# Layer 1's gate and up products in seven half-size products for eight, and adaLN columns moved beside down products and merges

## The chip, the cores and the metric

The kernel runs on one core of one Trainium2 chip. The metric is the device time of one execution in microseconds (us), as the median of several runs. A profiled execution gives the trace from which rows are read. The engines are named as the profile names them: PE (TensorE), PEld (its weight loads), DVE (VectorE), ACT (ScalarE), POOL (GpSimd), SP (SyncE, which issues most transfers).

## The reference

Two layers run over 640 tokens of width 1024: 128 context tokens and 512 latent tokens, with shared weights. Scale, shift and gate of each sublayer (adaLN) come from one vector for the context and one for the latents, by a product with `w_mod` (9 x 1024 columns a layer). Everything is float32.

```
h = rms(x, g_pre0) * (1 + c0) + s0
x = x + 0.5 * g0 * rms((silu(h @ Wg0) * (h @ Wu0)) @ Wd0, g_post0)
h = rms(x, g_pre1) * (1 + c1) + s1
x = x + g1 * rms(mixer(h), g_post1)
h = rms(x, g_pre2) * (1 + c2) + s2
x = x + 0.5 * g2 * rms((silu(h @ Wg1) * (h @ Wu1)) @ Wd1, g_post2)
```

Wg and Wu are 1024 x 2816, Wd is 2816 x 1024. The mixer holds a gated linear recurrence, an S5 state space branch and windowed attention; three gated branches are merged and multiplied by `w_out`.

## The kernel before

**Products.** Every large product is made in three matmuls (`mm3`, lines 91 to 95): each operand is split (`split`, lines 97 to 101) into a rounded high part, by a ScalarE cast (L100), and the rest, by a VectorE subtraction (L101), and high x high, high x low and low x high are summed in PSUM. A weight slab of 128 x 1024 (512 KB) is loaded by SP (`slab`, line 72) and split in two halves of 512 columns; six pairs of buffers hold split halves ahead of their use.

**The FFN** (`ffn`, lines 400 to 472). The 2816 hidden columns are 22 blocks of 128. For each block gate and up are made with the hidden columns on the partitions and the tokens as moving columns, in two parts of 384 and 256 tokens (`HALF`), 8 k-tiles each. tanh, two VectorE steps (L434, L435) and a split make the hidden block. The blocks come in two phases of 11; after each, the down product sums 11 blocks into five PSUM banks (five token tiles of 128), for one half of 512 output columns after the other. The first phase's sums are copied by ScalarE to an SBUF tile, `part`; the second phase's are added to it.

```
            for nh in range(2):
                ps = [self.mm() for _ in range(NT)]
                STG = self.STG[0] if (ch == 1 and nh == 1) else 0
                for jj in range(JC - STG):
```

**From one sublayer to the next.** In the last half (`nh == 1`) the last `STG` weight halves (8 in the FFN, 7 in the mixer) are held back, and then used token tile by token tile, so that a tile is finished while PE works on the next. For a finished tile `post_half` (lines 368 to 378) adds the part, squares (L376) and multiplies by the gate row (L377); `post` (from line 380) adds to x (L387; for tiles 2 to 4 half of it by ScalarE and POOL, L389 and L390); `prenorm` (lines 305 to 316) squares x (L310), takes the root on POOL (L300), multiplies by the row `A` = (1 + c) g_pre (L313 on VectorE, L314 on ScalarE, L315 on POOL); `turn` transposes the tile on PE (L327), adds the shift and splits it into the next sublayer's h (L331, L337, L338). The turns of tiles 3 and 4 wait until the next sublayer's first gate and up products of 384 tokens are under way (`flush`, line 348); one more gate product stands behind it.

**adaLN.** `mod_tile` (lines 247 to 258) loads 128 columns of `w_mod` (512 KB) and makes their dot products with the two SiLU rows on VectorE, four multiply-and-sum instructions over 512 elements (L255, each with a read of the accumulator) and two small additions (L258). `rows` (line 264) turns gate and scale columns into rows through a transpose, a DRAM tensor and two POOL transfers. `plan` (lines 500 to 511) lays the columns on the 22 gate and up steps of each FFN (48 in each layer's first FFN, 24 and 8 in the second ones); in layer 0 the S5 preparation lies on the same steps. `silu_rows` makes the SiLU rows anew in each of the four FFNs.

**Order.** Instructions are written in program order, and a planner with a cost model then orders them on each engine; the order on SP is kept as written. Every engine works its queue in order, so an instruction that waits holds up those behind it. Buffers are rings: `pp` (22 tiles of 128 x 640), `hp` (h), `wp`, `bg` (two tiles of 128 x 1024, which hold `w_mod` columns and normalized tiles), `xp`, `rawp`.

## Time and profile before

| | us |
|---|---|
| median of 3 runs | 3217.41 (3217.2 to 3219.97) |
| the profiled execution | 3221.69 |
| its span in the trace | 3219.9 |
| PE busy in the span | 3115.6 |
| DVE busy | 2006.3 |
| ACT busy | 1246.0 |
| POOL busy | 664.8 |

The span runs from the first to the last instruction; the execution's own time is 1.8 us longer. The rows below come from that one execution. A busy time on PE is modelled from pipelined matmuls, so what one matmul costs in a stream is read from the starts of many. Times of stretches are counted from the span's start. The span's order is: layer 0 first FFN to about 525, mixer to 1140, second FFN to 1635; layer 1 first FFN to 2107, mixer to 2721, second FFN to the end.

### The profile page before, as it was taken

How to read it: one execution, taken by the hardware profiler on the slowest of the kernel's cores; microseconds unless marked ns; L12 is line 12 of the kernel's file. 1: busy time of each engine (PE TensorE's matmuls, PEld its weight loads, DVE VectorE, ACT ScalarE, POOL GpSimd, SP SyncE). 2: the span in 40 equal slices, each digit the busy share in tenths (PEclk: the TensorE clock that was granted, in tenths of full speed). 3: DMA queues.
4: the chain of work that ended last, by engine and by line, in shares of the span. 5: the costliest groups of instructions: out<-in, count | busy, mean ns of one | idle time of the engine just before them, and what ended most of it. 6: DMA issues, size and time to landing. Idle time of an engine off the chain costs nothing.

```text
span 3219.9 us, 52039 instructions
## 1 busy us (share of the span) xinstructions
PE 3115.6 (97%) x19981; PEld 2908.8 (90%) x19981; DVE 2006.3 (62%) x4548; ACT 1246.0 (39%) x2757; POOL 664.8 (21%) x933
## 2 busy tenths in 40 slices
PE   7889999999999999999999999999999999999998
PEld 6788997879999989989989999977989998998997
DVE  6994886656735479737679648667565444642443
ACT  4222324475634353322252223246655433422232
POOL 2630002119820037200020000020594101100000
PEclk9999999999999999999999999999989999999999
DMA  6355444231452333524445334434215423422222
GB/s 241 116 184 171 158 158 161 82 77 63 95 151 73 125 125 122 193 98 144 149 146 171 130 112 158 157 119 86 76 56 125 129 72 135 148 86 85 86 99 86
DMA packets 138106, 398.45 MB, mean 124 GB/s; under 512 B 34704, under 2 KB 43424, under 8 KB 135424
## 3 DMA queue, kind: packets, MB, share of 16 engines
q1 hardware_dynamic: 127680, 362.37, 34.8%
q0 software_dynamic: 9456, 31.43, 3.0%
q8 instruction: 157, 2.57, 0.3%
q10 hardware_dynamic: 720, 1.31, 0.1%
q14 instruction: 93, 0.76, 0.1%
HBM read 355.77 MB, written 44.40 MB: 124 GB/s over the span
## 4 chain that ended last, share of the span: by engine, by line
PE 80%; DVE 10%; POOL 4%; issue 3%; ACT 2%; DMA 0%; POOLq 0%; DVEq 0%; SPq 0%; ACTq 0%
PE mm L93 24%; PE mm L94 24%; PE mm L95 24%; DVE wlo L101 1%; DVE junk L255 1%; PE mm L1252 1%; DVE x L387 1%; POOL s5t L1019 1%; PE mm L1241 1%; POOL H L1020 1%; POOL s5t L1018 1%; POOL s5t L1017 1%; PE mm L990 1%; ACT n L310 1%; PE mm L1216 1%
## 5 line engine op out<-in xcount | busy, mean ns | idle before, releaser
L94 PE MATMUL mm<-h,whi 128*128 128x384 f32 (+1 forms) x3968 | 1231.3, 311 | 8.8 <-DVE s L296 5.8
L95 PE MATMUL mm<-h,wlo 128*128 128x384 f32 (+1 forms) x3968 | 1230.4, 311 | 8.2 <-DVE wlo L101 8.2
L93 PE MATMUL mm<-h,whi 128*128 128x384 f32 (+1 forms) x3968 | 1229.7, 312 | 5.4 <-ACT h L337 2.0
L101 DVE TENSOR_TENSOR wlo<-raw,whi 128x512 fp32r<-128x512 f32 x780 | 570.7, 735 | 535.8 <-ACT whi L100 529.8
L94 PEld LDWEIGHTS mm<-h,whi 128*128 128x128 f32 x3968 | 758.5, 191 | 11.6 <-DVE s L296 6.5
L100 ACT CAST whi<-raw 128x512 fp32r<-128x512 f32 x780 | 477.2, 619 | 749.5 <-PE mm L95 382.2
L95 PEld LDWEIGHTS mm<-h,wlo 128*128 128x128 f32 x3968 | 757.9, 191 | 9.5 <-DVE wlo L101 9.5
L93 PEld LDWEIGHTS mm<-h,whi 128*128 128x128 f32 x3968 | 756.3, 191 | 10.8 <-ACT h L337 3.0
L93 PE MATMUL mm<-whi,P 128*128 128x512 f32 x980 | 381.6, 391 | 1.9 <-DVE tmp L434 1.9
L94 PE MATMUL mm<-wlo,P 128*128 128x512 f32 x980 | 381.7, 390 | 0.0
L95 PE MATMUL mm<-whi,P 128*128 128x512 f32 x980 | 381.1, 390 | 0.0
L255 DVE SCALAR_TENSOR_TENSOR junk<-wmod,W 128x512 bf16<-128x512 f32 x512 | 357.7, 699 | 10.0 <-DMA wmod<-w_mod 4.1
L281 POOL DMA_DIRECT2D gd<-grow x6 | 3.2, 528 | 1498.5 <-ACT grow L279 1258.2
L100 ACT CAST P<-tmp 128x384 fp32r<-128x384 f32 x192 | 88.2, 460 | 431.1 <-DVE tmp L435 429.7
L93 PEld LDWEIGHTS mm<-whi,P 128*128 128x128 f32 x980 | 184.0, 188 | 40.6 <-DVE tmp L434 2.4
L95 PEld LDWEIGHTS mm<-whi,P 128*128 128x128 f32 x980 | 184.0, 188 | 38.2
L94 PEld LDWEIGHTS mm<-wlo,P 128*128 128x128 f32 x980 | 184.1, 188 | 37.5
L433 ACT ACTIVATE tmp<-mm 128x384 f32<-128x384 f32 (+1 forms) x176 | 76.5, 435 | 224.6 <-PE mm L95 224.5
L95 PE MATMUL mm<-P,wlo 128*128 128x384 f32 (+1 forms) x512 | 158.8, 310 | 0.0
L94 PE MATMUL mm<-P,whi 128*128 128x384 f32 (+1 forms) x512 | 158.1, 309 | 0.0
L93 PE MATMUL mm<-P,whi 128*128 128x384 f32 (+1 forms) x512 | 158.0, 309 | 0.0
L817 DVE SCALAR_TENSOR_TENSOR tmp<-tmp,mm 128x384 f32<-128x384 f32 x64 | 31.0, 485 | 184.9 <-PE mm L95 92.6
(333 smaller groups left out, 4021.4 us busy)
## 6 DMA issues: line engine op xcount, KB each, us to landing
wmod<-w_mod SPq DMA_DIRECT2D x128, 512.0 KB, 3.5
raw<-w_gate SPq DMA_DIRECT2D x88, 512.0 KB, 3.5
raw<-w_up SPq DMA_DIRECT2D x88, 512.0 KB, 3.5
raw<-w_down SPq DMA_DIRECT2D x88, 512.0 KB, 3.5
raw<-w_in_fm SPq DMA_DIRECT2D x72, 512.0 KB, 3.5
xd<-x SPq DMA_DIRECT2D x25, 512.0 KB, 2.6
x<-xd SPq DMA_DIRECT2D x24, 512.0 KB, 4.4
W<-gd POOLq DMA_DIRECT2D x11, 1024.0 KB, 7.0
```

Source lines behind the costliest of these rows:

```text
L93: nc.tensor.matmul(ps, whi, ahi, start=first, stop=False)
L94: nc.tensor.matmul(ps, whi, alo, start=False, stop=False)
L95: nc.tensor.matmul(ps, wlo, ahi, start=False, stop=last)
L100: nc.scalar.copy(hi, src)
L101: return nc.vector.tensor_tensor(lo, src, hi.bitcast(F32), ALU.subtract)
L255: nc.vector.scalar_tensor_tensor(out=jk, in0=w[:, h * 512:(h + 1) * 512], scalar=1.0, in1=rows[c][h], op0=ALU.mult, op1=ALU.mult, accum_ou ...
L310: nc.scalar.activation(n, x, AF.Square, scale=1.0 / 32.0, accum_out=ss)
L387: nc.vector.scalar_tensor_tensor(out=x[:, hs], in0=f[h], scalar=rs, in1=x[:, hs], op0=ALU.mult, op1=ALU.add)
L433: nc.scalar.activation(t, pg[:, :n], AF.Tanh, scale=0.5)
L990: nc.tensor.matmul(pv[:, g], m1[:, g, ri], U[:, 4 * i + g], start=True, stop=True)
L1017: v.tensor_tensor(t[:, 0, :ns], cur, ar, ALU.mult)
L1018: v.tensor_tensor(t[:, 1, :ns], cur[:, :, ::-1], ai, ALU.mult)
```

## The change

- **Gate and up of layer 1.** In both FFNs of layer 1 the weight blocks are taken in 11 pairs. The first pair is computed as before, in parts of 320 tokens. For the other ten, each matrix of 1024 x 256 is cut into 2 x 2 quarters (512 x 128) and the tokens into 2 x 2 quarters (512 x 320), and seven products of quarters or of sums of quarters replace eight (`seven`). The token sums T1, T3, T2 are made on VectorE (`combine`) and T4 in `combine4`. The weight sums are made by accumulating transfers that POOL issues: two while loading (s, A21), two from one SBUF tile to another (A11 + s, A12 + A11). The seven products are added to four results with ScalarE copies and VectorE additions.
- **Three phases.** The second FFN of layer 0 and both of layer 1 take the blocks in phases of 6, 8 and 8. The sums of the first two phases are copied to SBUF (`put`), written and accumulated in DRAM by POOL, and read back in the last. Before a sublayer with paired products `STG` is 6 (`stage`), and at most one less than the phase's blocks.
- **adaLN columns.** In layer 1, 24 columns of the first FFN stand at the 28 down steps of its first two phases, 24 at the merges of two branches, and the last 8 (and the LRU output) at the second FFN's down steps (`spread`). A column is made by two instructions over 1024 elements for four over 512. The SiLU rows are made once.
- **Norms.** `prenorm` multiplies by the root alone; `turn` applies scale and shift as columns after the transpose. Turns of tiles 0 to 2 are issued two tiles later (`turn_next`), those of 3 and 4 at the next `flush`. `rows` makes the gate rows alone, by four smaller transfers into `pp` tiles.
- **Buffers.** h lies in `wp`, now 7 tiles; the memory for the descriptors of POOL's transfers is set to 8192.

```diff
+PHASES = {(0, 0): (11, 11), (0, 1): (6, 8, 8), (1, 0): (6, 8, 8), (1, 1): (6, 8, 8)}
+PAIRED = ((1, 0), (1, 1))
+PLAIN = tuple((l, i) for l in range(2) for i in range(2) if (l, i) not in PAIRED)
...
-        self.hp = pool("hp", 4)
         self.pp = pool("pp", 22)
-        self.wp = pool("wp", 3)
+        self.wp = pool("wp", 7)
...
-        rows = []
-        w = self.W_()
+        w = self.cp.tile([P, 2, 1024], F32, name="srows")
...
     def mod_tile(self, l, col, rows):
...
-        acc = self.S_(4)
+        m = self.mod[l]["mm"][:, :, col]
         for c in range(2):
-            for h in range(2):
-                jk = self.sm.tile([P, 512], BF16, tag="junk", name=self.nm("junk"), bufs=1)
-                nc.vector.scalar_tensor_tensor(out=jk, in0=w[:, h * 512:(h + 1) * 512], scalar=1.0,
-                                               in1=rows[c][h], op0=ALU.mult, op1=ALU.mult,
-                                               accum_out=acc[:, 2 * c + h:2 * c + h + 1])
-            nc.vector.scalar_tensor_tensor(out=self.mod[l]["m"][c][:, col:col + 1], in0=acc[:, 2 * c:2 * c + 1],
-                                           scalar=acc[:, 2 * c + 1:2 * c + 2], in1=self.mod[l]["b"][:, col:col + 1],
-                                           op0=ALU.add, op1=ALU.add)
+            jk = self.small("junk").bitcast(BF16)
+            nc.vector.scalar_tensor_tensor(out=jk, in0=w, scalar=1.0, in1=rows[:, c], op0=ALU.mult, op1=ALU.mult,
+                                           accum_out=m[:, c:c + 1])
+        nc.vector.tensor_tensor(m, m, self.mod[l]["b"][:, col:col + 1].to_broadcast([P, 2]), ALU.add)
...
+        nc.tensor.transpose(ps[:16, :P], s, self.ident)
...
+        nc.gpsimd.dma_start(d.rearrange("c (k p) -> (c k) p", p=P), g[:16])
+        out["G"] = []
+        for c in range(2):
+            w = [self.P_(shape=[P, 512]) for _ in range(2)]
+            for h in range(2):
+                nc.gpsimd.dma_start(w[h], d[c:c + 1, 512 * h:512 * h + 512].to_broadcast([P, 512]))
+            out["G"].append(w)
         return out
...
+        sq = nc.scalar.activation(n, x, AF.Square, scale=1.0 / 32.0, accum_out=ss)
         rs = self.rstd(ss)
-        self.norm = (
-            v.scalar_tensor_tensor(out=n[:, :512], in0=x[:, :512], scalar=rs, in1=R["A"][ci][0], op0=ALU.mult, op1=ALU.mult),
-            nc.scalar.mul(n[:, 512:], x[:, 512:], rs))
-        self.last_n = nc.gpsimd.tensor_tensor(n[:, 512:], n[:, 512:], R["A"][ci][1], ALU.mult)
-        self.turn(t, n, R, hT)
+        self.norm = (v.tensor_scalar(n, x, rs, None, ALU.mult), sq)
+        def turn():
+            self.turn(t, n, R, hT)
+        (self.turns if t < 3 else self.late).append(turn)
...
+    def turn_next(self, t):
+        if t >= 2 and self.turns:
+            self.turns.pop(0)()
...
+                nc.tensor.transpose(ps[:, i * P:(i + 1) * P], n[:, (4 * q + i) * P:(4 * q + i + 1) * P], self.ident)
+            h = n[:, q * 512:(q + 1) * 512].rearrange("p (k t) -> p k t", k=4)
+            for i in range(4):
+                k = slice(4 * q + i, 4 * q + i + 1)
+                o = ps[:, i * P:(i + 1) * P]
+                if i % 2:
+                    v.tensor_scalar(h[:, i], o, a[:, k], b[:, k], ALU.mult, ALU.add)
+                else:
+                    nc.scalar.activation(h[:, i], o, AF.Identity, scale=a[:, k], bias=b[:, k])
+            hs.append(h)
...
-                for i in range(4):
-                    o, b = ps[:, i * P:(i + 1) * P], B[:, 4 * q + i:4 * q + i + 1]
-                    nc.scalar.activation(hi[:, i], o, AF.Identity, bias=b)
-                    d = v.scalar_tensor_tensor(out=lo[:, i], in0=o, scalar=b, in1=hi[:, i].bitcast(F32),
-                                               op0=ALU.add, op1=ALU.subtract)
-            if t < 3:
-                self.turned = d
+                d = self.split(hi, lo, h)
+        if hT.paired:
+            for c, n_, half, o in self.PIECES[t]:
+                h, cs = [h[:, :, c:c + n_] for h in hs], slice(o, o + n_)
+                d = self.quarters(hT, h, half, cs)
+                if half:
+                    self.todo.append(lambda h=h, cs=cs: self.combine(hT, h, cs))
+            if t == 2:
+                self.combos()
...
+    PIECES = {0: [(0, 128, 0, 0)], 1: [(0, 128, 0, 128)], 2: [(0, 64, 0, 256), (64, 64, 1, 0)],
+              3: [(0, 128, 1, 64)], 4: [(0, 128, 1, 192)]}
...
+    def combine(self, hT, hs, cs):
+        v = self.nc.vector
+        T = {k: (z[:, 0, :, cs], z[:, 1, :, cs]) for k, z in hT.t.items()}
+        h12, h22 = hs
+        n = cs.stop - cs.start
+        t1 = self.tmp.tile([P, 512], F32, tag="tmp", name=self.nm("tc"))[:, :4 * n].rearrange("p (k t) -> p k t", k=4)
+        f = lambda x: x.bitcast(F32)
+        v.tensor_tensor(t1, f(T["B11"][0]), h12, ALU.subtract)
+        v.tensor_tensor(t1, t1, f(T["B11"][1]), ALU.add)
+        self.split(*T["T1"], t1)
+        v.tensor_tensor(h12, h22, h12, ALU.subtract)
+        self.split(*T["T3"], h12)
+        v.tensor_tensor(t1, t1, h22, ALU.add)
+        self.split(*T["T2"], t1, -1.0)
+    def combine4(self, hT):
+        v = self.nc.vector
+        t, f = hT.t, lambda x: x.bitcast(F32)
+        del t["B12"]
+        z = t["T4"] = self.wp.tile([P, 2, 4, TH], F32R, tag="W", name=self.nm("hT4"))
+        for y in range(2):
+            k = slice(2 * y, 2 * y + 2)
+            w = self.P_().rearrange("p (k t) -> p k t", k=2)
+            v.tensor_tensor(w, f(t["T2"][:, 0, k]), f(t["B21"][:, 0, k]), ALU.add)
+            v.tensor_tensor(w, w, f(t["T2"][:, 1, k]), ALU.add)
+            v.tensor_tensor(w, w, f(t["B21"][:, 1, k]), ALU.add)
...
-                STG = self.STG[0] if (ch == 1 and nh == 1) else 0
-                for jj in range(JC - STG):
...
+                STG = min(n - 1, self.stage(self.STG[0], hTn)) if (final and nh == 1) else 0
+                for jj in range(n - STG):
...
+                    if dram and final and nh == 0 and jj == 0:
+                        part = self.new_part()
+                        for t in range(NT):
+                            nc.gpsimd.dma_start(part[t].whole, self.pd[t])
...
+                    self.background(("down", ch, nh, jj))
...
-                    if ch == 0:
-                        nc.scalar.copy(part[t][nh], ps[t])
-                    else:
+                        jj = n - STG + r
+                        self.mm3(ps[t], hid[jj][0][:, ts], hid[jj][1][:, ts], whi, wlo, jj == 0, jj == n - 1)
+                    if final:
...
+    def put(self, t, nh, ps, ch):
+        nc = self.nc
+        k = (5 * nh + t) % 4
+        o = (self.xp if k % 2 else self.bg).tile([P, 512], F32, tag="x" if k % 2 else "bg", name=self.nm("put"))
+        nc.scalar.copy(o, ps)
+        d = self.pd[t][:, nh * 512:nh * 512 + 512]
+        if ch:
+            nc.gpsimd.dma_start(d, o, accum_op=ALU.add)
+        else:
+            nc.gpsimd.dma_start(d, o)
...
+    def paired(self, l, i, hT):
...
+        first(0, 0, 0)
+        first(0, 1, 0)
+        self.flush()
+        product(0, 0)
+        first(1, 0, 0)
+        first(1, 1, 0)
+        product(1, 0)
+        for f in range(2):
+            first(f, 0, 1)
+            first(f, 1, 1)
+            product(f, 1)
+            self.combos()
+        self.combine4(hT)
+        st = [self.rawp.tile([P, 1024], F32, tag="raw", name=self.nm("raw")) for _ in range(2)] + [self.P_(shape=[P, 512])]
+        extra = self.seven(W[0, 1], st, hT.t)
+        next(extra)
+        yield hid[0]
+        yield hid[1]
...
+        sets = [[big[:, o:o + 1024], big[:, o + 1024:o + 2048], big[:, o + 2048:o + 2560]] for o in (0, 2560)]
...
+                    g = self.seven(W[m, jp], sets[m], hT.t)
+                    next(g)
+                out = next(g)
...
+                        if m == 0:
+                            t = self.tmp.tile([P, 512], F32, tag="tmp", name=self.nm("tmp"))[:, :TH]
+                            nc.scalar.activation(t, z, AF.Tanh, scale=-0.5 if f else 0.5)
+                            v.scalar_tensor_tensor(out=z, in0=t, scalar=1.0, in1=z, op0=ALU.add, op1=ALU.mult)
+                        else:
+                            y = gate[f][:, h * TH:(h + 1) * TH]
+                            v.scalar_tensor_tensor(out=z, in0=z, scalar=0.5, in1=y, op0=ALU.mult, op1=ALU.mult)
+                            self.prod = self.split(*(x[:, h * TH:(h + 1) * TH] for x in hid[f]), z)
...
+    def seven(self, src, st, T):
+        nc, v, g = self.nc, self.nc.vector, self.nc.gpsimd
+        x, y, s = st
+        a11, a12, a21, a22 = x[:, :512], x[:, 512:], y[:, :512], y[:, 512:]
+        add = lambda o, a: g.dma_start(o, a, accum_op=ALU.add)
+        nc.sync.dma_start(x, src[:, :1024])
+        nc.sync.dma_start(s, src[:, 1024:1536])
+        self.last_slab = nc.sync.dma_start(y, src[:, 1024:])
+        add(s, src[:, 1536:])
+        add(a21, src[:, :512])
+        yield
+        out = [self.P_(), self.P_()]
+        o = [[z[:, h * TH:(h + 1) * TH] for h in range(2)] for z in out]
+        def product(ps, a, b, more=False):
+            whi, wlo = self.parts(a)
+            for k in range(4):
+                cs = slice(k * P, (k + 1) * P)
+                for e, (w, z) in enumerate(((whi, 0), (whi, 1), (wlo, 0))):
+                    nc.tensor.matmul(ps[:, :TH], w[:, cs], T[b][:, z, k], start=not more and k == e == 0,
+                                     stop=k == 3 and e == 2, skip_group_check=more)
+        yield out
+        pa, pb = self.mm(), self.mm()
+        product(pa, a11, "B11")
+        nc.scalar.copy(o[0][0], pa[:, :TH])
+        add(a11, s)
+        product(pb, a12, "B21")
+        v.tensor_tensor(o[0][0], o[0][0], pb[:, :TH], ALU.add)
+        add(a12, a11)
+        yield [(0, 0)]
+        pe, pf = self.mm(), self.mm()
+        product(pe, s, "T1")
+        nc.scalar.copy(o[1][1], pe[:, :TH])
+        product(pf, a21, "T3")
+        v.tensor_tensor(o[1][1], o[1][1], pf[:, :TH], ALU.add)
+        product(pa, a11, "T2", True)
+        nc.scalar.copy(o[0][1], pa[:, :TH])
+        nc.scalar.copy(o[1][0], pa[:, :TH])
+        v.tensor_tensor(o[1][1], o[1][1], pa[:, :TH], ALU.add)
+        yield [(1, 1)]
+        product(pe, a12, "B22", True)
+        v.tensor_tensor(o[0][1], o[0][1], pe[:, :TH], ALU.add)
+        yield [(0, 1)]
+        product(pf, a22, "T4", True)
+        v.tensor_tensor(o[1][0], o[1][0], pf[:, :TH], ALU.add)
+        yield [(1, 0)]
+    def stage(self, n, hT):
+        return 6 if hT is not None and hT.paired else n
...
+    def spread(self, l, i, fs):
+        slots = [("down", ch, nh, jj) for ch, n in enumerate(PHASES[l, i][:-1]) for nh in range(2) for jj in range(n)]
+        q = {}
+        for k, f in enumerate(fs):
+            q.setdefault(slots[k * len(slots) // len(fs)], []).append(f)
+        return q
...
+                if nh == 1:
+                    self.turn_next(t)
...
+            for f in self.mixq.pop((br, j), ()):
+                f()
...
-            self.plan(self.s5_prep(0) if l == 0 else [], modq(l, range(16, 64)), 0 if l else 3)
+            if (l, 0) in PAIRED:
+                self.bgq = self.spread(l, 0, modq(l, range(16, 40)))
+                self.mixq = {}
+                for x, f in enumerate(modq(l, range(40, 64))):
+                    self.mixq.setdefault((0, x // 2) if x < 16 else (1, x - 16), []).append(f)
+            else:
+                self.plan(self.s5_prep(0), modq(l, range(16, 64)), 3)
...
-                self.plan([(7, self.lru_out)], modq(l, range(64, 72)), 0)
+                self.bgq = self.spread(l, 1, modq(l, range(64, 72)) + [self.lru_out])
...
-    nc = bacc.Bacc("TRN2", target_bir_lowering=False, num_devices=1)
+    nc = bacc.Bacc("TRN2", target_bir_lowering=False, num_devices=1, dynamic_dma_scratch_size=8192)
```

## Rows read from the trace of the kernel before

**Rows 1.** The page's totals: busy us, share of the span, instructions.
```profile
PE 3115.6 (97%) x19981; PEld 2908.8 (90%) x19981; DVE 2006.3 (62%) x4548; ACT 1246.0 (39%) x2757; POOL 664.8 (21%) x933
```

**Rows 2.** Stretches: length, busy us per engine (instructions), granted clock, DMA share, GB/s.
```profile
120.00:240.00 120.00, 104.57 (x871) 99.49 (x872) 119.55 (x255) 32.53 (x75) 48.81 (x41) 0.96 0.51 171
...
1680.00:1800.00 120.00, 120.00 (x821) 120.00 (x820) 106.20 (x294) 38.35 (x75) 0.00 (x0) 1.00 0.50 163
1840.00:1880.00 40.00, 40.00 (x178) 33.11 (x178) 8.30 (x12) 10.33 (x17) 0.00 (x0) 1.00 0.28 93
...
2440.00:2720.00 280.00, 280.00 (x1873) 273.58 (x1872) 121.97 (x225) 107.03 (x219) 33.66 (x66) 1.00 0.40 116
...
1634.00:1674.00 40.00, 34.76 (x174) 30.12 (x174) 34.53 (x64) 24.83 (x56) 18.62 (x18) 0.91 0.52 175
1654.00:1674.00 20.00, 14.76 (x78) 13.50 (x77) 18.53 (x38) 14.70 (x37) 9.98 (x9) 0.83 0.69 219
```

**Rows 3.** PE in order of time, 1700 to 1712: start us, us, line, tiles.
```profile
1701.52 0.28 PE L93 MATMUL mm<-h,whi 128*128 128x256 f32 x1
...
1707.26 0.34 PE L93 MATMUL mm<-h,whi 128*128 128x384 f32 x1
...
1711.95 0.33 PE L93 MATMUL mm<-h,whi 128*128 128x384 f32 x1
```

**Rows 4.** Groups by shape, 3000 to 3080, gate and up: busy us, mean ns.
```profile
L101 DVE TENSOR_TENSOR wlo<-raw,whi 128x512 fp32r<-128x512 f32 x24 | 16.6, 692 | 9.9 <-ACT whi L100 9.9
L255 DVE SCALAR_TENSOR_TENSOR junk<-wmod,W 128x512 bf16<-128x512 f32 x8 | 5.5, 688 | 0.1
L101 DVE TENSOR_TENSOR P<-tmp,P 128x384 fp32r<-128x384 f32 x6 | 3.3, 558 | 3.5 <-ACT P L100 3.5
...
L434 DVE SCALAR_TENSOR_TENSOR tmp<-tmp,mm 128x384 f32<-128x384 f32 x5 | 2.8, 554 | 9.8 <-ACT tmp L433 9.8
...
L101 DVE TENSOR_TENSOR P<-tmp,P 128x256 fp32r<-128x256 f32 x6 | 2.5, 418 | 0.0
L434 DVE SCALAR_TENSOR_TENSOR tmp<-tmp,mm 128x256 f32<-128x256 f32 x6 | 2.5, 412 | 0.0
L258 DVE SCALAR_TENSOR_TENSOR mod<-s,bmod 128x1 f32<-128x1 f32 x4 | 0.9, 216 | 0.1
L255 DVE DVE_READ_ACCUMULATOR junk<-wmod,W 128x1 f32 x8 | 0.7, 82 | 0.0
...
L100 ACT CAST whi<-raw 128x512 fp32r<-128x512 f32 x24 | 14.9, 620 | 14.6 <-PE mm L94 11.2 <-ACT tmp L433 3.4
```

**Rows 5.** Transfers by line: issuing queue, count, KB each, median us to landing.
```profile
raw<-w_gate SPq DMA_DIRECT2D x88, 512.0 KB, 3.5
...
W<-gd POOLq DMA_DIRECT2D x11, 1024.0 KB, 7.0
...
m1d<-W POOLq DMA_DIRECT2D x16, 512.0 KB, 4.8
...
ud<-ut POOLq DMA_DIRECT2D x8, 320.0 KB, 3.2
```

**Rows 6.** Waits of PE, 1610 to 1690: us in total, times, longest.
```profile
PE mm L94 <- DVE h L338: 3.0, 1, 3.0
PE mm L93 <- ACT h L337: 2.0, 1, 2.0
```

**Rows 7.** Groups by shape, 1630 to 1675, a change of sublayer: busy us, mean ns.
```profile
L338 DVE SCALAR_TENSOR_TENSOR h<-mm,mod,h 128x128 fp32r<-128x128 f32 x19 | 5.8, 343 | 0.4 <-ACT h L337 0.3
L101 DVE TENSOR_TENSOR wlo<-raw,whi 128x512 fp32r<-128x512 f32 x6 | 5.4, 932 | 0.2 <-ACT whi L100 0.2
...
L315 POOL TENSOR_TENSOR n<-n,W 128x512 f32<-128x512 f32 x5 | 6.9, 1385 | 2.6 <-ACT n L314 2.6
```

**Rows 8.** Line L255 alone (VectorE), 120 to 240: length, busy us (instructions), clock, DMA, GB/s.
```profile
120.00:240.00 120.00, 44.51 (x111) 0.96 0.51 171
```

More of the change, by code (lines that the diff above doesn't have):

```diff
@@ new lines, in rows @@
+            a = self.sm.tile([P, 2, 8], F32, tag="acol", name=self.nm("acol"), bufs=2)
+            for c in range(2):
+                v.scalar_tensor_tensor(out=a[:, c], in0=self.mod[l]["m"][c][:, (3 * ph + 1) * 8:(3 * ph + 2) * 8],
+                                       scalar=1.0, in1=self.mod[l]["gpre"][:, ph * 8:ph * 8 + 8], op0=ALU.add, op1=ALU.mult)
+            out["A"] = [a[:, c] for c in range(2)]
+            out["B"] = [self.mod[l]["m"][c][:, 24 * ph:24 * ph + 8] for c in range(2)]
@@ new lines, in quarters @@
+    def quarters(self, hT, hs, half, cs):
+        for q in range(2):
+            z = hT.t[("B11", "B21", "B12", "B22")[2 * half + q]]
+            d = self.split(z[:, 0, :, cs], z[:, 1, :, cs], hs[q])
+        return d
+    def combine(self, hT, hs, cs):
[12 more added lines that the diff above has]
+        self.split(*T["T2"], t1, -1.0)
@@ L439, in ffn @@
+        phases = PHASES[l, i]
+        part = None
+        dram = len(phases) > 2
+        hidden = self.paired(l, i, hT) if hT.paired else self.plain(l, i, hT, first)
+        it = iter(self.down_halves(l, i))
+        for ch, n in enumerate(phases):
+            hid = [next(hidden) for _ in range(n)]
+            final = ch == len(phases) - 1
+            if not dram and not final:
                 part = self.new_part()
-            else:
-                hTn = None if last else self.new_hT()
+            if final:
+                next(hidden, None)
+                hTn = None if last else self.new_hT(nxt[1] != 1 and (nxt[0], nxt[1] // 2) in PAIRED)
```

289 lines of the change are left out of this document (173 added, 116 removed).

## The prediction

> **What bounds the kernel now.** I read the totals first, then stretches of 20 to 120 us, then single matmul starts, then mean durations by shape, then waits. TensorE is busy 3115.6 us of a span of 3219.9 [rows 1]. The stretches say where it is truly the bound: in layer 1's first gate and up (1680 to 1800) and in a down stage (1840 to 1880) it has no gap and full clock, while VectorE is busy 106.2 of 120 us in the one and 8.3 of 40 in the other [rows 2]. So matmuls taken out of gate and up shorten the run as long as VectorE keeps up. Two stretches go the other way: 120 to 240 (layer 0, S5 preparation beside gate and up), where VectorE is full and TensorE short by 120 - 104.57 = 15.4 us; and each change from one sublayer to the next (1634 to 1674), where VectorE is busy 34.5 of 40 us and TensorE waits [rows 2].
>
> The reader should see in the matmul starts what one costs in a stream: 48 of 256 columns take 1707.26 - 1701.52 = 5.74 us, 0.1196 each; 27 of 384 take 4.69 us, 0.1737 each [rows 3]. A matmul of 320 columns lies midway: 0.1467 us.
>
> **The matmuls.** A "unit" is one matrix (gate or up) of one pair of 128-column blocks. Before: 48 matmuls of 384 and 48 of 256 columns, 48 x (0.1737 + 0.1196) = 14.08 us. After: 7 products x 4 k-tiles x 3 = 84 of 320 columns, 84 x 0.1467 = 12.32 us. Each unit saves 1.76 us. Layer 1 has 2 FFNs x 10 pairs x 2 matrices = 40 such units (the first pair of each FFN stays at eight products): **-70.3 us**. A 1% error of the midpoint is 5 us. Down keeps all its matmuls; three phases for two change their order alone.
>
> **VectorE beside a pair (24.64 us of TensorE).** 14 half-slab subtractions for 8: 14 x 0.692 = 9.7; ten additions of a product to a result, not there before, 10 x 0.483 (320 columns, between the 554 and 412 ns of the gate step): 4.8; eight gate and up steps 8 x 0.483 = 3.9; four hidden subtractions 4 x 0.488 = 2.0 [rows 4]. Sum 20.4, 83% of the unit's time. From 1680 to 1800 VectorE stood at 88% and TensorE lost nothing [rows 2], so I cost it at 0. ScalarE casts 14 x 0.620 = 8.7 us [rows 4] and, with copies, tanh and hidden casts of about 0.45 each, stays below VectorE. The adaLN columns that filled VectorE there must leave, and do.
>
> **Weight sums.** Four accumulating transfers of 256 KB a unit, issued by POOL, are in no row. Three of them stand in series on one buffer set: the sum s, then A11 + s (after A11 was split), then A12 + A11, after which the set may be loaded again. Two sets serve alternate units, so a round may last 24.64 us: loads 5 (512 KB lands in 3.5, and 1.25 MB is asked), three sums of L, one split of 1.3 (620 and 692 ns). It fits if L < (24.64 - 6.3)/3 = 6.1 us. The nearest rows are POOL's plain transfers: 512 KB lands in 4.8 us, 1024 KB in 7.0 [rows 5]. A sum reads 256 KB twice and writes it once, so I take 4.8: round 20.7 us, cost 0. The ends are 3.2 (ud, 320 KB) and 7.0, which would cost 3 x 0.9 us in each of 20 rounds, 54 us. Queued behind a late sum on POOL are the next unit's sums; ScalarE and VectorE wait for it in the split, and with them every later evacuation. [...]
>
> The Trainium skill, DMA: Bandwidth & Descriptors, "Anatomy of one DMA - SWDGE (gpsimd) path", fits such a transfer as 2.0 us plus bytes at 436 GB/s: 2.6 us for 256 KB as an estimate, by which the sums could never be late and the slower rival below would have no place. The rows here speak against that fit: it gives 3.2 us for 512 KB, where the trace has 4.8 [rows 5]. The Trainium skill, Collectives: The Full Stack, "The bandwidth ceiling", says that an add in the transfer reads two sources and so runs at half a copy's rate; no row of before shows it.
>
> **The start of a paired FFN** (twice: after layer 0's second FFN and after layer 1's mixer). Before, TensorE waits 5.0 us there for h, and the clock granted from 1654 to 1674 is 0.83, between its levels of 1.2 and 2.4 GHz, after that wait [rows 2, 6]. VectorE sets the pace (18.53 of 20 us busy). New work on it: the token sums T1, T3, T2 take 7 operations per piece. The 64-token piece (256 elements, 0.418 each) gives 2.9 us, inside the turn of tile 2; the two 128-token pieces (512 elements) 14 x 0.692 = 9.7; T4 takes 10 operations of 640 elements at 0.83 (0.692 + 128 x 1.07 ns, the slope between 256 and 512): 8.3 [rows 4]. A tile's turn itself stays: 4 x 0.343 and two splits of 0.692, 2.8 us, for 8 x 0.343 = 2.7 [rows 7].
> - Up to the first product of the later tokens: +2.9; less cover, since 6 halves instead of 8 (7 in the mixer) are kept for the tile-by-tile end, 2 x 3 x 0.225 = 1.35 us per tile (40/178 us a matmul of 512 [rows 2]) for the last three, +4.0 (mixer +2.0); four products of 24 x 0.1467 = 14.1 us in front instead of three of 4.17 = 12.5: -1.6. Makes +5.3 and +3.3.
> - From there to the seventh product of the first unit: VectorE 9.7 + 8.3 + 4 x 1.45 (hidden) + 7 x 0.692 + 3 x 0.48 = 30.0 us, TensorE 4 x 3.52 + 6 x 1.76 = 24.6: +5.4.
> - A second gap brings the low clock again: 20 x 0.17 = +3.4.
>
> Together 14.1 + 12.1 = **+26 us**. Ends: 0, where the planner fills VectorE's idle time and subtraction falls back from 932 ns (beside POOL's multiplications, which go) to 692 [rows 4, 7]; and 55, where nothing of 2 x 20.9 is hidden and cover and clock are added. I take the sum by operations.
>
> **adaLN columns.** One column takes 4 x 0.688 + 4 x 0.082 + 2 x 0.216 = 3.51 us of VectorE; with rows of 1024, 2 x (0.688 + 512 x 1.07 ns) + 2 x 0.082 + 0.2 = 2.84 [rows 4]. In layer 1, 24 go to 28 steps of the first two down phases: 0.692 + 24/28 x 2.84 = 3.1 of 15 x 0.225 = 3.37 us, hidden, but close. Their 512 KB loads stand in SP's queue before weight slabs and wait for one of two buffers, which the copies of the finished phase (ScalarE, then POOL to memory) now share. Ends: 0, and one column (2.8) at each of four phase ends, 11; I take **+5**. 24 more go beside the merges: VectorE 122 + 68 of 280 us [rows 2], cost 0; without that cover they would cost up to 68.
> In layer 0, 111/4 = 28 columns stand in 120 to 240 [rows 8]; 28 x 0.67 = 19 us less on a full VectorE. TensorE can gain 0 to 15.4; its waits there are for the S5 chain, which also waits for POOL, so **-6**.
>
> **Other sublayer changes.** POOL's 1.385 us multiplication leaves the chain, the turns are issued two tiles later, layer 1's first FFN keeps 7 halves for 8. Ends -6 and +6; **-2**. SiLU rows made once instead of four times, the moved row transfers, the part sums through memory: the LRU output moved to a down step (one transpose, one copy): beside TensorE; 0, and if a part came back late, one 4.8 us landing per FFN.
>
> **Sum.** -70.3 + 26 + 5 - 6 - 2 = -47 us. The profiled execution took 3221.69 us; the median of the runs is 4.3 us below it. Taken off the median, 3217.4 - 47 = **3170**.
>
> **Rivals.**
> 1. *The start is hidden.* For it: VectorE idles in the first 8 us of a change, and POOL's contention goes. Against: 18.53 of 20 us at its end. About 8 instead of 26, and +3 instead of +5: 3150. Chance 0.16.
> 2. *The sums are a little late*, L between 6.1 and 6.7: up to 36 us back, about 3195. For it: 4.8 and 7.0 enclose the bound. Chance 0.12.
> 3. *Slower: the sums set the pace.* Place: the round s, A11, A12 on one buffer set. Price: 3 us per us of L above 6.1, in 20 rounds, 60 us per us. It decides at L = 6.9, where the 47 are gone; at 7.2 the run takes 3236. For it: the sum is two reads and a write, and a wait in POOL's queue lengthens L for the next. Against: one 512 KB read is 4.8. Chance 0.12.
> 4. *VectorE swells beside POOL's descriptor work.* If every operation grew as subtraction did in the sublayer change (932 for 692), a pair would need 27.5 us: 20 x 2.9 = 58 back. Against: POOL has no two-input work here. A part of it, 3195 to 3200. Chance 0.08.
> That seven products don't save an eighth is excluded by the count of columns.
>
> **How the numbers follow.** Forecast 0.52 (3150 to 3192 by its own bounds), the rivals 0.16, 0.12, 0.12, 0.08. About 0.2% (6.4 us) is what a measurement can tell here. Slower 0.12; same 0.04, from the edges of 2 to 4; faster 0.84. The range 3140 to 3212 takes in the forecast, 1, most of 2 and 4, and leaves out 3.
>
> **What would show it.** 40 x 12 = 480 matmuls fewer in gate and up; a unit of 12.3 us with no gap; a POOL sum's landing below 6.1 us; VectorE near 83% in units; gaps of about 10 us in all at each paired start. Wrong: waits of the splits for a weight sum, or TensorE idle inside units.

## The result: 3323.59 us, and the profile after

The median of 4 runs is 3323.59 us (3323.23 to 3333.22), against 3218.12 us of the kernel before in the same series: ratio 1.0334, 95% interval 1.0315 to 1.0353. The forecast was 3170, and the range (3140 to 3212) does not hold the result.

The page's first line after, to be held against [rows 1]:

```profile
PE 3105.8 (94%) x19501; PEld 2880.7 (87%) x19501; DVE 2088.2 (63%) x4256; ACT 1380.7 (42%) x3066; POOL 832.1 (25%) x1156
```

The 480 matmuls are gone (19981 to 19501). At the price of a stream (columns at 2.4 GHz and 13 ns for each matmul, which gives the durations of [rows 3]) a unit has 3840 columns and 12 matmuls less to do. That is 1.76 us, or 70.2 over 40 units: the saving that the sum went by. But TensorE stands still longer: 215.9 us of the span (3321.7 - 3105.8) for 104.3 before. Its three largest waits over the run, by what it waited for (us in total, times, longest):

```profile
PE mm L671 <- ACT whi L105: 50.8, 20, 7.4
PE mm L671 <- ACT P L677: 34.4, 17, 3.9
PE mm L334 <- DVE n L315: 29.8, 6, 8.8
```

L671 is the matmul of the seven products: the first row waits for the split of a weight sum (31.9 us of it in front of the T2 or B22 product, 18.9 in front of T1 in the first unit of each FFN), the second for a copy of a finished product out of PSUM (L677). L334 is the transpose of a normalized tile at a change of sublayer. Three stretches (columns as in [rows 2]): the first four units of layer 1, seven later units of the same FFN, and the change into layer 1:

```profile
1701.00:1782.00 81.00, 64.25 (x369) 60.90 (x368) 59.26 (x116) 31.72 (x68) 12.96 (x15) 0.87 0.66 165
2018.00:2126.00 108.00, 95.52 (x599) 92.36 (x599) 63.25 (x128) 47.54 (x105) 23.41 (x29) 0.95 0.60 140
1634.00:1674.00 40.00, 27.61 (x128) 23.73 (x127) 30.22 (x65) 23.60 (x53) 11.49 (x12) 0.79 0.48 159
```

In the second stretch TensorE idles inside the units (12.5 of 108 us) while VectorE is busy 59% of the time; the forecast had 83%. After such waits the granted clock is below full too (0.95 and 0.87, between its levels of 1.2 and 2.4 GHz), so the gaps cost more than their length. The third stretch, at 0.79, holds the start of the FFN, a term of its own in the forecast. From the first matmul of a unit to the end of its last, the 40 units take 12.5 to 26.0 us (median 16.3, sum 659). How one comes to that length is seen on POOL's timeline, where every instruction is a weight sum (`raw<-raw`: onto A11 or A12; `raw<-w_pair`: the two early ones, for T1 and T3; columns: start, us, engine, line, tiles, idle time before and what ended it):

```profile
2061.86 0.86 POOL L656 DMA_DIRECT2D raw<-raw  x1 [3.85 <-DVE wlo L106]
...
2068.56 0.86 POOL L656 DMA_DIRECT2D raw<-raw  x1 [0.38 <-issue]
...
2078.48 0.86 POOL L656 DMA_DIRECT2D raw<-raw  x1 [4.55 <-DVE wlo L106]
...
2084.36 0.86 POOL L656 DMA_DIRECT2D raw<-raw  x1 [0.47 <-DMA raw<-raw]
```

The first is one unit's sum onto A11, the second its sum onto A12, issued when the first has landed; the third is the *next* unit's sum onto A11, 16.62 us after the first. It waits for a split. ScalarE in the same time:

```profile
2068.13 0.62 ACT L105 CAST whi<-raw 128x512 fp32r<-128x512 f32 x1 [3.65 <-DMA raw<-raw]
...
2074.04 0.62 ACT L105 CAST whi<-raw 128x512 fp32r<-128x512 f32 x1 [4.93 <-DMA raw<-raw]
...
2075.44 0.42 ACT L677 COPY P<-mm 128x320 f32<-128x320 f32 x1
...
2083.93 0.62 ACT L105 CAST whi<-raw 128x512 fp32r<-128x512 f32 x1 [2.10 <-DMA raw<-raw]
```

At 2074.04 the cast of A12 waits for its sum; the casts of the next unit's first quarters stand behind it, and so does the copy at 2075.44, without which the T2 product can't start in its bank. PE, whose T2 weights were cast at 2068.13, stops for it:

```profile
2075.91 0.56 PE L671 MATMUL mm<-hT,whi 128*128 128x320 f32 x2 [3.13 <-ACT P L677]
```

Over all units, from issue to landing a sum onto A11 or A12 takes 5.2 us (median), the second is issued 0.5 after the first has landed, and the next unit's first 4.4 after that: 5.2 + 0.5 + 5.2 + 4.4 = 15.3 us for TensorE's 12.5. The median unit is 1.0 us longer than this; that part was not taken apart.

```profile
raw<-w_pair SPq DMA_DIRECT2D x88, 512.0 KB, 5.4
raw<-w_pair POOLq DMA_DIRECT2D x78, 256.0 KB, 4.3
raw<-raw POOLq DMA_DIRECT2D x78, 256.0 KB, 5.2
```

These are transfers after (issuing queue, count, KB, median us to landing), to be read beside [rows 5].

### The profile page after: what moved, and what is told of

It is laid out like the page before. It is cut to its first block, busy times and chain, and to the rows that moved or that the text cites. A ratio compares the mean times of both kernels' runs of the same rounds, so it can differ in the third digit from the quotient of the medians.

```text
span 3321.7 us, 51922 instructions
## 1 busy us (share of the span) xinstructions
PE 3105.8 (94%) x19501; PEld 2880.7 (87%) x19501; DVE 2088.2 (63%) x4256; ACT 1380.7 (42%) x3066; POOL 832.1 (25%) x1156
## 3 DMA queue, kind: packets, MB, share of 16 engines
q0 software_dynamic: 41712, 91.70, 12.9%
## 5 line engine op out<-in xcount | busy, mean ns | idle before, releaser
L106 DVE TENSOR_TENSOR wlo<-raw,whi 128x512 fp32r<-128x512 f32 x901 | 642.3, 720 | 639.1 <-ACT whi L105 630.5
L98 PE MATMUL mm<-h,whi 128*128 128x256 f32 (+1 forms) x2560 | 796.1, 313 | 7.2 <-ACT h L105 4.5
L100 PE MATMUL mm<-h,wlo 128*128 128x256 f32 (+1 forms) x2560 | 794.5, 311 | 5.0 <-DVE wlo L106 4.9
L99 PE MATMUL mm<-h,whi 128*128 128x256 f32 (+1 forms) x2560 | 795.3, 311 | 0.0
L98 PEld LDWEIGHTS mm<-h,whi 128*128 128x128 f32 x2560 | 488.6, 191 | 12.2 <-ACT h L105 4.9
L100 PEld LDWEIGHTS mm<-h,wlo 128*128 128x128 f32 x2560 | 489.3, 191 | 7.0 <-DVE wlo L106 6.9
L99 PEld LDWEIGHTS mm<-h,whi 128*128 128x128 f32 x2560 | 489.9, 191 | 1.8 <-issue 1.2
L259 DVE SCALAR_TENSOR_TENSOR junk<-wmod,srows 128x1024 bf16<-128x1024 f32 x256 | 317.1, 1239 | 77.7 <-DMA wmod<-w_mod 76.5
L671 PE MATMUL mm<-hT,whi 128*128 128x320 f32 x1280 | 300.1, 324 | 55.5 <-ACT P L677 34.4
L671 PEld LDWEIGHTS mm<-hT,whi 128*128 128x128 f32 x1280 | 225.0, 199 | 63.3 <-ACT P L677 39.3
L671 PE MATMUL mm<-hB,whi 128*128 128x320 f32 x960 | 231.4, 331 | 33.4 <-ACT whi L105 31.6
L671 PEld LDWEIGHTS mm<-hB,whi 128*128 128x128 f32 x960 | 173.1, 204 | 42.9 <-ACT whi L105 37.1
L671 PE MATMUL mm<-hT,wlo 128*128 128x320 f32 x640 | 203.0, 320 | 0.0
```

The costliest lines, as they stand in the source:

```text
L98: nc.tensor.matmul(ps, whi, ahi, start=first, stop=False)
L99: nc.tensor.matmul(ps, whi, alo, start=False, stop=False)
L100: nc.tensor.matmul(ps, wlo, ahi, start=False, stop=last)
L106: return nc.vector.tensor_tensor(lo, src, hi.bitcast(F32), ALU.subtract)
L259: nc.vector.scalar_tensor_tensor(out=jk, in0=w, scalar=1.0, in1=rows[:, c], op0=ALU.mult, op1=ALU.mult, accum_out=m[:, c:c + 1])
L671: nc.tensor.matmul(ps[:, :TH], w[:, cs], T[b][:, z, k], start=not more and k == e == 0, stop=k == 3 and e == 2, skip_group_check=more)
```

## The experiments

**Theory 1**: the sums onto A11 and A12 are in series in every unit, since ScalarE's queue holds the next A11 split behind the split that waits for A12; the round is two landings and the splits. **Theory 2**: the DMA engines are too full with accumulating traffic (their share is 0.60 to 0.66 above). **Theory 3**: VectorE or ScalarE set the pace. **Theory 4**: the number of split buffers, or the planner's order of products. In the quotations theories go by these numbers. Each series ran the kernel before beside it (3218.43 to 3220.16).

### Which sums cost: e1_no_serial and e2_no_early

```diff
 e1_no_serial
-        add(a11, s)
-        add(a12, a11)
 e2_no_early
-        add(s, src[:, 1536:])
-        add(a21, src[:, :512])
```

> Leaves out the two sums that stand in series in a unit (the one onto A11 and the one onto A12), so the products with T2 and B22 use raw quarters. Theory 1 (the two serial accumulating transfers and the splits between them make the round of every unit): the gaps inside units go, units last 12.4 to 13.5 us but for the first of each half, and the time falls by 120 to 160 us to 3165 to 3205. Theory 2 (the DMA engines are too full): half of the accumulating bytes are gone, units still 14 to 15 us, time 3240 to 3280. Theory 3 (VectorE or ScalarE set the pace): no change, 3310 to 3325. Theory 4 (the number of split buffers, the order of the products): 3290 to 3325.

> Leaves out the other two sums instead (those onto the T1 and T3 weights, issued ahead), the same bytes as in the run without the serial ones. Theory 1: the chain of A11 and A12 stays, units still last 14 to 17 us, and the time is 3285 to 3325; only the first unit of each half may lose its gap of 7 us. Theory 2: as fast as the run without the serial sums, both 3240 to 3280. Theories 3 and 4: no change, 3300 to 3325.

Measured: 3198.39 and 3260.32 us (one run each). Without the serial sums 29 of 40 units last 12.48 us, and of the waits above little is left (all but 1.1 us in the first unit of each FFN):

```profile
PE mm L671 <- ACT whi L105: 13.1, 4, 7.0
PE mm L671 <- ACT P L677: 1.1, 1, 1.1
```

Its units in layer 1's first FFN:

```profile
1957.00:2062.00 105.00, 103.87 (x696) 102.62 (x695) 78.21 (x155) 59.14 (x124) 17.49 (x22) 1.00 0.59 155
```

TensorE is all but full with the DMA share as high as in the change (0.59). Without the early sums the units stay at 14.3 us (median), as theory 1 has it, but the time fell by 63 us, more than it allowed. The transfers of that run show why:

```profile
raw<-raw POOLq DMA_DIRECT2D x78, 256.0 KB, 4.3
```

The serial sums land in 4.3 instead of 5.2 us once the early ones are gone, and the round holds two of them: 2 x 0.9 = 1.8 of the 2.0 us by which the median unit became shorter. So the early transfers lengthen the links of the chain (a part of theory 2), and the chain is what makes it count. The other way it does not show: without the serial sums the early ones landed no sooner (4.3 in the change), as e1 has it:

```profile
raw<-w_pair POOLq DMA_DIRECT2D x78, 256.0 KB, 4.5
```

### The sums on an engine: e3_serial_pool, e5_serial_vec, e8_all_vec

```diff
 e3_serial_pool (e5_serial_vec: v.tensor_tensor)
-        add(a11, s)
+        g.tensor_tensor(a11, a11, s, ALU.add)
-        add(a12, a11)
+        g.tensor_tensor(a12, a12, a11, ALU.add)
 e8_all_vec, as e5 and
-        nc.sync.dma_start(s, src[:, 1024:1536])
-        add(s, src[:, 1536:])
+        v.tensor_tensor(s, a21, a22, ALU.add)
-        add(a21, src[:, :512])
+        v.tensor_tensor(a21, a21, a11, ALU.add)
```

> The two serial sums are made by GpSimd on the tiles instead of by accumulating transfers; the two early ones stay transfers. Theory 1: a sum takes some 1.4 us in place of 4.9 to 5.3 to its landing, the chain of a unit falls below 12.3 us, units last 12.4 to 13.5 us, time 3165 to 3200. Theory 2: DMA load as in the run without the serial sums, time 3240 to 3280. Theory 3: GpSimd's added work slows VectorE, time above 3300.

> The two serial sums by VectorE (0.69 us each by its 512-wide additions) where the GpSimd version took 1.5 to 1.6 us each and VectorE's own operations beside it became longer (the final multiplication of a unit 823 ns for 487). Theory 1: units at 12.48 us; VectorE's share of a unit rises from about 70 to 81 per cent without being stretched; time 3200 to 3213, 5 to 15 us below the GpSimd version's 3216.75. If the GpSimd version lost nothing to GpSimd's additions, 3213 to 3220; if VectorE is too full for them, above 3225.

> All four weight sums by VectorE from the loaded quarters: no accumulating transfer and no second load of the lower left quarter, two loads of 512 KB a unit. VectorE at about 92 per cent of a unit. If what is left of the early sums' traffic still costs (the gap of 7 and 5 us in the first unit of each half, the clock), 3190 to 3205; if VectorE is then the bound, units 12.8 to 14 us and 3215 to 3250.

Measured: 3216.75 us with GpSimd (ratio to before 0.9988, 0.9979 to 0.9997), 3210.12 with VectorE (0.9971, 0.996 to 0.9982), 3230.45 with all four on VectorE (1.0041, 1.0027 to 1.0054). Two small additions in place of two transfers give back 107 and 113 us. Both medians of a unit are 12.48 us. With them on VectorE that engine has more to do than in the change, and ScalarE is busy 58.76 of 105.00 us in units, so theory 3 falls. The GpSimd version missed its 3165 to 3200: its 40 units sum to 551 us, for 535 in e1 and 541 with VectorE. GpSimd's additions also hold up VectorE. Its groups by shape in units of layer 1's second FFN (busy us, mean ns):

```profile
L106 DVE TENSOR_TENSOR wlo<-raw,whi 128x512 fp32r<-128x512 f32 x55 | 47.5, 869 | 11.1 <-ACT whi L105 8.8 <-PE mm L671 1.9
L638 DVE SCALAR_TENSOR_TENSOR P<-tmp,P 128x320 f32<-128x320 f32 x16 | 10.5, 659 | 0.0
```

and the same two groups with the sums on VectorE:

```profile
L106 DVE TENSOR_TENSOR wlo<-raw,whi 128x512 fp32r<-128x512 f32 x55 | 37.8, 688 | 13.7 <-ACT whi L105 13.2
L638 DVE SCALAR_TENSOR_TENSOR P<-tmp,P 128x320 f32<-128x320 f32 x16 | 7.8, 486 | 0.0
```

In these eight units TensorE is full all the same (100.00 of 100 us in both runs); the longer units of the GpSimd version lie elsewhere, and what the longer operations cost was not measured apart.

With all four sums on VectorE the first units of the two FFNs are no better (23.5 and 20.7 us, for 22.9 and 21.6 in e5): the wait for a load goes, and waits for VectorE's splits come. Units become 13.2 us (median), though VectorE shows 55.73 of 67.00 us busy. In the last phase TensorE waits before T4 for the addition that reads its bank (L687):

```profile
PE mm L671 <- DVE P L687: 3.4, 4, 1.1
```

### The same transfers in another order: e12_a11_ahead

The next unit's loads, its A11 split and its sum onto A11 are issued inside the running unit, behind T2 and ahead of B22 and T4 (not across a down stage). Nothing is removed, and the number of split buffers stays.

```diff
         add(a21, src[:, :512])
         yield
+        first = self.parts(a11)
+        add(a11, s)
+        yield
...
                 for done in g:
+                    if m == 0 or jp not in ends:
+                        if done == [(0, 0)]:
+                            ahead = self.seven(W[1 - m, jp + m], sets[1 - m], hT.t)
+                            next(ahead)
+                        elif done == [(1, 1)]:
+                            next(ahead)
...
-        add(a11, s)
```

> The changed kernel with all four accumulating transfers of every unit, and only the order of issue moved: inside a down phase's run of units, the loads of the next unit and its split of A11 with the sum onto A11 are issued right behind the T2 product of the running unit, ahead of its splits for B22 and T4. Theory 1 (the two sums are in series within every unit because the split of the next A11 stands behind the split that waits for the sum onto A12): the two landings of neighbouring units overlap, most units 12.5 to 14 us, time 3220 to 3260 for 3323.6. Theory 2 (the transfers as such, the load on the DMA engines, or the chain of POOL's queue): same bytes, same transfers, so units stay at 14 to 18 us and the time at 3300 to 3330.

Measured: 3235.07 us (ratio to before 1.0044, 1.0029 to 1.0059), 88.5 us less than the change. Transfers and a stretch of this kernel:

```profile
raw<-w_pair POOLq DMA_DIRECT2D x78, 256.0 KB, 4.7
raw<-raw POOLq DMA_DIRECT2D x78, 256.0 KB, 5.4
```

```profile
2018.00:2078.00 60.00, 60.00 (x407) 59.74 (x406) 43.71 (x87) 33.47 (x71) 14.94 (x19) 1.00 0.71 181
```

The landings are no shorter (5.4 us), the DMA share is higher (0.71) and TensorE is full. What went is the 4.4 us between one unit's sum onto A12 landing and the next sum onto A11 being issued: now 0.2 in the median. The loads and the two early sums move ahead as well, but in the change they were not what ScalarE's splits waited for:

```profile
ACT whi L105 <- DMA raw<-raw: 234.3, 60, 7.5
ACT whi L105 <- DMA raw<-w_pair: 3.5, 2, 1.9
```

In e12 the first of these is 107.3 us. So theory 2 falls as the main cause, and theory 1 stands. Theory 4 was right in this only: the order is the cause, by the queue it leaves on ScalarE. Of the 40 units 18 last 12.48 us and 21 are above 12.6 (sum 566, for 659 in the change). Ten of the 21 are first in a phase, where nothing was issued ahead, or last in one; the others have single waits of up to 2.2 us, for copies and splits of ScalarE and VectorE.

### The rest of the change: e4_no_products, e6_turns_now, e7_cols_before, e10_old_norm, e11_col_halves, e14_two_phases

```diff
 e4_no_products
-PAIRED = ((1, 0), (1, 1))
+PAIRED = ()
...
 e6_turns_now, as e4 and
-        (self.turns if t < 3 else self.late).append(turn)
+        turn() if t < 3 else self.late.append(turn)
 e7_cols_before, as e4 and
-                self.bgq = self.spread(l, 0, modq(l, range(16, 40)))
+                self.plan([], modq(l, range(16, 64)), 0)
...
 e10_old_norm, as e7, with rows, prenorm and turn of the kernel before
 e11_col_halves, as e7, with mod_tile in two halves of 512
 e14_two_phases, as e10 and
-PHASES = {(0, 0): (11, 11), (0, 1): (6, 8, 8), (1, 0): (6, 8, 8), (1, 1): (6, 8, 8)}
+PHASES = {(0, 0): (11, 11), (0, 1): (11, 11), (1, 0): (11, 11), (1, 1): (11, 11)}
```

(e4 and those on it keep layer 1's spread columns until e7 takes them back; e7 also undoes the columns 64 to 71 and the LRU output in the second FFN.)

> All of the change but the seven products: layer 1's gate and up as eight plain products again, with the new normalising, the turns placed behind, the three down phases through memory and the spread adaLN columns. If the rest of the change costs what the traces seem to show (4.5 us in layer 0, some 10 us in mixer 1, a few at each boundary), 3225 to 3245; if it brings what was forecast of it (3 us less), 3205 to 3220.

> The kernel without the seven products, with the turns of the first three token tiles issued at once again in place of two tiles later (the new normalising stays). If the late turns are what the five boundaries pay for (3 to 6 us each), 3230 to 3238 for 3247.16; if it is the work of VectorE in the new turns and not their place, 3243 to 3250.

> The kernel without the seven products, with layer 1's adaLN columns back beside gate and up of its two FFNs in place of down products and mixer merges. By the segments of the two traces the columns beside the merges cost some 6 us (VectorE busy 40.0 of 40 us there) and those beside down products some 1 to 3: 3237 to 3242 for 3247.16. If they cost nothing there, 3245 to 3250.

> The kernel without the seven products and with the columns where they were (3235.35), and the normalising and turns of before: the scale as a broadcast row, halves of the work on VectorE, ScalarE and GpSimd, turns at once. If the new normalising on VectorE alone costs the boundaries, 3218 to 3226; if what is left (17 us over before) lies in the phases through memory or the wider adaLN columns, 3231 to 3238.

> The kernel without the seven products and with the columns where they were (3235.35), each adaLN column again in two 512-wide products and a combination for one 1024-wide one. If the wide form costs layer 0's first FFN its 4 to 7 us, 3229 to 3233 and that FFN ends 4 us earlier; if not, 3233 to 3240.

> The kernel without the seven products, with the columns and the normalising of before (3227.36), and all four FFNs in two down phases with their partial sums on the chip, as before the change. If the third phase through memory holds what is left over the kernel before, 3217 to 3222; if it costs nothing, 3225 to 3230.

| kernel | us | ratio to before (interval) |
|---|---|---|
| e4_no_products | 3247.16 | 1.0084 (1.0067 to 1.0101) |
| e6_turns_now | 3248.64 | 1.0095 (1.0078 to 1.0112) |
| e7_cols_before | 3235.35 | 1.0053 (1.0038 to 1.0068) |
| e11_col_halves | 3234.20 | 1.0046 (1.0031 to 1.0060) |
| e10_old_norm | 3227.36 | 1.0024 (1.0014 to 1.0034) |
| e14_two_phases | 3219.46 | 1.0005 (0.9995 to 1.0014) |

What was forecast as a gain of 3 us costs 28, and the steps take it back: 11.8 for the columns' place, 8.0 for the normalising, 7.9 for the third phase (differences of medians from different series; by the ratios 10, 9 and 6 us, each known to some 4 to 7). TensorE's idle time in the traces falls along with them: 125.3 us in e4, 112.9 in e7, 104.6 in e10, 97.0 in e14. Neither the place of the turns nor the 1024-wide column has an effect that can be told. e4, e7 and e10 came out 1 to 2 us outside the ranges expected for them. Where the columns go: merges of mixer 1 in e4 (first row), and with the columns back beside gate and up in e7 (second):

```profile
2570.00:2610.00 40.00, 36.46 (x244) 35.49 (x243) 40.00 (x84) 18.02 (x36) 0.00 (x0) 1.00 0.54 179
```

```profile
2560.00:2600.00 40.00, 40.00 (x280) 40.00 (x280) 24.72 (x47) 21.09 (x42) 0.00 (x0) 1.00 0.24 76
```

Two columns a step fill VectorE (40.00 of 40) where the mean over 280 us [rows 2] had shown room. The normalising shows at the changes of sublayer: from 20 us before the first write of x to 60 after it, at each of the five, TensorE idles 44.6 us in all in e7 and 32.5 in e10. And the third phase: waits of PE at the entry of mixer 1, with three phases (e10) and with two (e14):

```profile
PE mm L333 <- DVE n L314: 7.1, 1, 7.1
PE mm L333 <- POOL n L316: 1.1, 1, 1.1
```

```profile
PE mm L100 <- DVE h L344: 2.5, 2, 1.8
PE mm L99 <- DVE wlo L106: 1.4, 2, 1.1
PE mm L333 <- POOL n L316: 0.2, 1, 0.2
```

That is 8.2 for 4.1 us. At the end of layer 0's second FFN, TensorE idles 7.8 us of such a stretch for 5.2; elsewhere the two runs hardly differ.

With 8 blocks in the last phase 7 halves at most are held for the end, and the parts come from memory; which of the two makes the first transpose late was not separated.

### Versions below the kernel before: e9_cols_early and e13_old_norm_mix

Both stand on e5_serial_vec. e9 moves columns 40 to 55 to mixer 0's merges; e13 adds the old normalising at the three boundaries that don't lead into a paired FFN.

```diff
-                    self.mixq.setdefault((0, x // 2) if x < 16 else (1, x - 16), []).append(f)
+                self.mixq = {(0, x): [f] for x, f in enumerate(modq(1, range(56, 64)))}
...
+                self.mixq = {(x // 8, x % 8): [f] for x, f in enumerate(modq(1, range(40, 56)))}
```

> The version with the serial sums on VectorE (3210.12) and layer 1's adaLN columns 40 to 55 moved from mixer 1's merges into those of mixer 0, one to a step, the other eight staying at one a step. If the columns crowded at two a step beside mixer 1's merges cost the 6 us that the segments show, mixer 1 goes from 625 to 617 to 620 us and the time to 3201 to 3207; if mixer 0 pays the same, 3207 to 3213.

> The version with serial sums on VectorE and the columns spread over both mixers (3206.18), with the normalising of before at the three boundaries that do not lead into a paired FFN. If the 8 us of the other run hold here too, of which about two thirds lie at these boundaries, 3198 to 3203; if they were given back elsewhere, 3204 to 3209.

Measured: 3206.18 us (0.9956, 0.9942 to 0.9971) and 3204.65 (0.9953, 0.9937 to 0.9970). Mixer 1 went from 625.4 to 620.3 us (first write of x to first write of x), mixer 0 paid 2 of it. e13 gained nothing that can be told from e9, where some 5 us were expected; where they went was not looked for. With what is left of the rest beside them, the seven products come out 14 us below the kernel before, not 47.

## Why the prediction was wrong

The runs are a ladder from the change to the kernel before, so its steps can be laid beside the terms of the sum (the first two steps rest on a single run of e1, and the last two are known to some us only):

| term | forecast | measured |
|---|---|---|
| matmuls and start of the paired FFNs | -70.3 + 26 = -44 | 3198.39 - 3247.16 = -49 |
| weight sums | 0 | 3323.59 - 3198.39 = +125 |
| adaLN, layer 1 | +5 | 3247.16 - 3235.35 = +12 |
| adaLN, layer 0 | -6 | about 0 (e11, and e14, which keeps the wide columns) |
| other sublayer changes, phases | -2 | 3235.35 - 3219.46 = +16 |

**The step that failed** is in "Weight sums": "Two sets serve alternate units, so a round may last 24.64 us", with three sums and one split in it, and from that "It fits if L < (24.64 - 6.3)/3 = 6.1 us". The size was nearly right (L taken at 4.8, measured 4.3 for the early sums and 5.2 for the two between tiles), and by the rule it fitted; the sign that the forecast named for it, a landing below 6.1 us, came true. The rule was wrong. Two buffer sets let two rounds overlap only if the queues let them: the working asked when a set comes free, and never wrote down the order of ScalarE's queue, in which the split of unit n's A12 stands ahead of the split of unit n+1's A11. With it the round is one unit's: 2 L + 0.5 + 4.4 < 12.5, so it fits only below L = 3.8. Put in the forecast's own form, as an estimate, at 5.2 it costs 2 x 1.4 us in each of 40 units, 112 us of the 125 measured. The sentence that ScalarE and VectorE "wait for it in the split, and with them every later evacuation" described the very wait (L671 on L677, 34.4 us), as a remark and not as a term. e12 shows how far the forecast's rule holds once the order allows it: with the same transfers and L = 5.4, 18 of 40 units last 12.48 us, and the median is 12.85.

**Rival 3** named the place (the sums set the pace; the round of s, A11 and A12) but not the order of the queue. It put its point at L = 6.9 by the same rule, so it got 0.12, and its slope was 60 us per us of L where two landings in each of 40 units make 80.

**The price by the page.** The Trainium skill, DMA: Bandwidth & Descriptors, "Anatomy of one DMA - SWDGE (gpsimd) path", gave 2.6 us as an estimate for 256 KB; the accumulating transfers landed in 4.3 to 5.4 us, so the measurement decides against that estimate here. The Trainium skill, Collectives: The Full Stack, "The bandwidth ceiling", has a transfer step that adds run at half the rate of one that copies, because it reads two sources. In the second stretch above the software queue, which holds the sums, stands against the hardware queue, which holds plain loads (packets, MB, share of 16 engines over 108 us):

```profile
q0 software_dynamic: 3907, 7.89, 38.6%
q1 hardware_dynamic: 2305, 7.08, 21.3%
```

Per MB that is 4.9 against 3.0 points of share, 1.6 times as much, although q0 also holds plain transfers. Packet by packet, a packet of 2048 bytes takes 178 ns (median) in the sums and 84 in plain loads of that stretch, 2.1 times as much; this trace agrees. It is the adding and not the queue: before, when q0 held plain transfers alone, the two queues were alike per MB over the span:

```profile
q1 hardware_dynamic: 127680, 362.37, 34.8%
q0 software_dynamic: 9456, 31.43, 3.0%
```

**What held.** 480 matmuls are gone, and a unit takes 12.48 us, for 12.32, when nothing is late. VectorE did no harm: the forecast had it at 83% in the units, and e1, with no sums on it, shows 78.21 of 105.00 us (74%), e5, with two sums more, 89.09 (85%). The start of a paired FFN and the matmuls came out at -49 for -44 together; no run measures the start by itself, so two errors may offset each other in it.

**What else failed.** The turns "issued two tiles later" stand in a term of -2: their place is indeed nothing (e6), but the normalising and the third phase, costed together at -2 and 0, are +16. "24 more go beside the merges: VectorE 122 + 68 of 280 us [rows 2], cost 0": a mean over 280 us hid 40 us that became full. "-6" in layer 0: the stretch 120 to 240 kept VectorE full (119.73 of 120 us) and TensorE short after the change as before, and halves for whole columns change nothing (e11). TensorE's wait for the S5 preparation is no shorter there (15.1 us for 12.9).

## What to carry to other kernels

This double-buffered chain could overlap two units only where each in-order queue on its way let it: before costing a wait at nothing, write down, for one unit, the order of the instructions on *every* engine the chain passes, and look for an early step of the next unit behind a late step of this one. Small sums between tiles that sit in such a chain were better made by an engine (0.69 us on VectorE) than by an accumulating transfer (5.2 us), and issuing the next unit's first link ahead was worth most of what a faster link was (88.5 us for 107 and 113). When a load is moved beside other work, look at the busiest 40 us of the new place, not at its mean.

## What the runs showed of the hardware

- An accumulating transfer of 256 KB between tiles landed in 5.2 us, and in 4.3 when the two early ones of the unit were left out (e2). The early ones landed in 4.3 us, and in 4.5 when the other two were left out (e1): the lengthening went one way, and its cause is not shown.
- TensorE can be full at a DMA share of 0.71 (e12, 60.00 of 60 us); the share as such did not slow it.
- A GpSimd addition of 128 x 512 can hold up a VectorE operation with two SBUF inputs until it ends. Over the 100 us of the groups above in e3, the 44 subtractions (L106) that overlap no addition take 686 ns in the mean; the 11 that overlap one take 0.97 to 2.52 us, and each ends about 0.55 us after that addition. Of eight gate and up steps (L638, L641) that overlap one, six had begun 0.14 to 0.18 us ahead of it and ran through in 0.48 to 0.49 us, and two took 1.58 and 2.13. A VectorE addition with one input in PSUM (L694) keeps its 0.49 us beside one:

```profile
3108.55 1.62 POOL L681 TENSOR_TENSOR raw<-raw 128x512 f32<-128x512 f32 x1
3108.21 2.52 DVE L106 TENSOR_TENSOR wlo<-raw,whi 128x512 fp32r<-128x512 f32 x1
...
3131.93 1.62 POOL L681 TENSOR_TENSOR raw<-raw 128x512 f32<-128x512 f32 x1
3132.29 0.49 DVE L694 TENSOR_TENSOR P<-P,mm 128x320 f32<-128x320 f32 x1 [0.42 <-PE mm L671]
```

The Trainium skill, GPSIMD Engine Reference, "1. Specifications", has its SBUF interfaces shared with VectorE, in contention with operations that have two SBUF inputs; this trace agrees.
